# Branch A's last tiles up to w_out: banks of the merged rows, place of the gate chunks' loads, divides and the order of w_out's first half

## The chip, the core and the metric

The kernel runs on one core of a Trainium2 chip. TensorE (PE) multiplies matrices into the eight banks of PSUM; ScalarE (ACT) and VectorE (DVE) read those banks and write SBUF; GpSimd (POOL) works on SBUF; SyncE (SP) issues the DMAs, whose packets are moved by 16 DMA engines. Each engine takes its own instructions in order and waits for the others by semaphores. The metric is the device time of one execution in microseconds.

## The reference

One layer of a bidirectional encoder over 1024 sample rows and 256 prompt rows of width 1024, in fp32. With the checks of masks and padding left out:

```python
h = rmsnorm(x, g_mix); z = h @ w_in
qa, ka, va = ...            # branch A: 8 heads of 64, 2 kv heads, window 128, with a sink
qb, kb, vb = ...            # branch B: 3 groups of 4 heads, dilations 1, 4, 16
gates = sigmoid(z[..., o6:] + b_gate).reshape(b, S, 2, D_MODEL)
o_a, _ = _banded_attention(qa, ka, va, A_WINDOW, 1, rel_bias[:, :A_HEADS], sink)
o_b = _dilated_mixture(qb, kb, vb, rel_bias[:, A_HEADS:])   # mixed by softmax of the groups' lse
merged = gates[:, :, 0] * (o_a @ w_branch_a) + gates[:, :, 1] * (o_b @ w_branch_b)
x = x + merged @ w_out
h = rmsnorm(x, g_mlp)
x = x + square(relu(h @ w_up)) @ w_down
y = rmsnorm(x, g_final)
```

## The kernel before

Rows come in ten tiles of 128 (eight of the sample, two of the prompt) and in three blocks of columns (512, 512, 256). Every product is made from two halves of each operand: a high part rounded to a shorter format by ACT (`hi`, an activation with Copy) and the rest as a low part by DVE (`lo`, a subtraction). `mm3` (L188 to L193) then adds three matmuls to a bank for each pair. PSUM has four kinds of banks: `mm` (3), `sc` (2), `pt` (2) and `pv` (1).

The stages that bear on the change, with their time in the profile: attention A (583 to 769 us), gates and branches (769 to 865), the first half of w_out's columns (865 to 920) and the second half (920 to some 996). Then come the MLP's entry, its up product (from some 1020) and its down product (to the end).

*Attention A* walks 40 steps `i`, one for each of four units and ten row tiles. A step issues the scores of its own tile (L1016 to L1024: matmuls into `sc`, then DVE for the row maximum, ACT for the exponent), the transposes of the tile before into `pt` (L1039), and the values of the one before that (L1053). Between them stand two fillers: `logits` (L1067), which computes five chunks of gate columns with `weight()` and stores them to DRAM (`gs`, `scr_g`), and the merges of branch B. A chunk's weights take three steps: `fetch` (L218) issues the DMA of `raw`, and `prepare` (L224) makes `whi` on ACT (L231) and `wlo` on DVE (L235). `weight()` prepares one chunk ahead of the one that it returns, and fetches within `prepare`. All raw, high and low chunks, the `gs` and the `r` rows come from one ring of ten buffers (`w`).

In steps 36 to 39 `turn_merged` (L1146) transposes a tile of branch B's merged rows into a `pt` bank (L1153) and copies it to `obhi` (ACT, L1161); `low_b` writes `oblo` (DVE, L1165), after which the bank is free. In steps 38 and 40 the weights of branch B are prepared, ahead of that step's scores.

*Gates and branches* are 48 jobs (L1294), each a product for one block and 128 columns into an `mm` bank: first eight of branch B, then four of branch A, for each block, and at the end the other four of branch A. Each is multiplied by a gate (`sg`, loaded from `scr_g` six jobs ahead, L1265; its sigmoid on ACT, L1270) into `mT` on DVE (L1319; for branch A L1321 and L1322). A table `side` (L1286) names what else each job issues: `divide` (L1176, a tile of branch A's rows by its sum), `turn_a` (L1185, its transposes into `pt`), `low_a`, `turn_merged` and `low_b` for the tiles from 4 on.

*w_out* multiplies tile by tile, 24 matmuls each; `part(t)` splits tile t of `mT` into `mhi` (ACT, L185) and `mlo` (DVE, L186), two tiles ahead. DVE adds the bank to the residual `x2`.

What sets the order: up to step 35, and again from job 40 through the first half of w_out, a scheduler orders the instructions of each engine; from step 36 to job 39, and from the second half of w_out on, they stand in the order in which the code issues them (`tc.manual_schedule`).

## Time and profile before

| what | value |
|---|---|
| median of three runs | 1791.44 us (1791.10 to 1794.48) |
| span of the profiled execution | 1788.8 us |
| granted TensorE clock, mean | 0.987 |
| TensorE busy | 1731.5 us (97%) |
| VectorE, ScalarE, GpSimd busy | 991.7, 714.1, 501.6 us |
| HBM read, written | 169.10 MB, 90.73 MB |

The profile's span runs from the first to the last recorded instruction of one execution, and the page has no other time of that execution; the three times are device times of executions without a profile, and their median is 2.64 us above the span. In timeline rows the columns are start and duration in us, engine, line, operation, output and inputs, and in square brackets the idle time ahead of the instruction and what ended it. A row of waits reads: engine, tile and line, what it waited for, then us in total, times and the longest. In a row of windows stand the stretch, its length, the busy time of PE, PEld, DVE, ACT and POOL (instructions in brackets), the granted clock, the mean share of the 16 DMA engines, and GB/s.

### The profile page before, as it was taken

To read this page: it belongs to the slowest core of one execution; us is meant where nothing else is said; L and a number is where in the kernel's file an instruction comes from. 1 tells how busy PE (TensorE), PEld (TensorE's weight loads), DVE (VectorE), ACT (ScalarE), POOL (GpSimd) and SP (SyncE) were. 2 spreads that over 40 slices of the span, in tenths; PEclk is the share of its full clock that TensorE was granted. 3 is DMA by queue.
4 is the path that set the end of the run, shared out by engine and by line. 5 is a ranking of instruction groups with operands and counts; after the bars stand their busy time and mean duration, and the time that the engine had idled before them with its cause. 6 is when DMAs were issued, how large, how long until landed. Compare 5 with 4: busy or idle time off the path is not lost.

```text
span 1788.8 us, 25229 instructions
## 1 busy us (share of the span) xinstructions
PE 1731.5 (97%) x9248; PEld 1466.8 (82%) x9248; DVE 991.7 (55%) x1683; ACT 714.1 (40%) x1531; POOL 501.6 (28%) x396
## 2 busy tenths in 40 slices
PE   7999999999999999999999799999999999999998
PEld 6898888777777889878888688888888788888886
DVE  6623333345545466566737655454554876667575
ACT  6232223344444355454426533333333433333345
POOL 0222321223322111100010255565555451315050
PEclk9999999989999999999999899999999999999999
DMA  6415335555455853164411144433444854623333
GB/s 230 144 37 165 108 105 147 143 147 146 138 161 143 252 158 103 61 241 142 190 47 82 54 140 150 148 118 121 140 150 169 299 199 142 241 95 117 127 113 118
DMA packets 218067, 256.26 MB, mean 143 GB/s; under 512 B 21455, under 2 KB 148771, under 8 KB 217816
## 3 DMA queue, kind: packets, MB, share of 16 engines
q1 hardware_dynamic: 209512, 232.32, 40.4%
q0 software_dynamic: 7344, 20.24, 3.4%
q10 hardware_dynamic: 1088, 2.10, 0.3%
q8 instruction: 73, 1.20, 0.3%
q14 instruction: 50, 0.41, 0.1%
HBM read 169.10 MB, written 90.73 MB: 145 GB/s over the span
## 4 chain that ended last, share of the span: by engine, by line
PE 61%; DVE 3%; ACT 2%; DMA 2%; issue 1%; POOL 0%; SPq 0%; ACTq 0%; DVEq 0%; POOLq 0%
PE dn L344 20%; PE mm L192 13%; PE x L344 10%; PE pv L344 5%; PE z L344 5%; PE y L344 2%; PE pv L1053 2%; PE pt L1039 1%; PE sc L1016 1%; PE sc L1017 1%; PE mm L344 1%; DMA raw<-in_w_down_dram 0%; DVE ulo L186 0%; PE pv L538 0%; DMA raw<-in_w_in_dram 0%
## 5 line engine op out<-in xcount | busy, mean ns | idle before, releaser
L344 PE MATMUL x<-chi,wlo 128*128 128x512 f32 x424 | 172.1, 406 | 6.9 <-ACT phi L185 6.9
L344 PE MATMUL dn<-dhi,ulo 128*128 128x512 f32 x448 | 174.6, 390 | 2.8 <-DVE ulo L186 2.8
L344 PE MATMUL dn<-dhi,uhi 128*128 128x512 f32 x448 | 174.3, 389 | 0.0
L344 PE MATMUL dn<-dlo,uhi 128*128 128x512 f32 x448 | 174.3, 389 | 0.0
L344 PE MATMUL x<-clo,whi 128*128 128x512 f32 x424 | 168.5, 397 | 0.0
L344 PE MATMUL x<-chi,whi 128*128 128x512 f32 x424 | 167.9, 396 | 0.0
L377 POOL TENSOR_TENSOR tb<-raw 128x512 f32<-128x512 f32 x30 | 39.0, 1302 | 453.6 <-PE mm L192 139.6
L311 DVE TENSOR_TENSOR wlo<-ta,whi 128x1024 fp32r<-128x1024 f32 x30 | 56.6, 1887 | 184.7 <-ACT whi L309 184.7
L311 DVE TENSOR_TENSOR wlo<-raw,whi 128x1024 fp32r<-128x1024 f32 x60 | 92.4, 1540 | 105.7 <-ACT whi L309 105.7
L344 PEld LDWEIGHTS dn<-dhi,ulo 128*128 128x128 f32 x448 | 84.1, 188 | 21.4 <-DVE ulo L186 3.8
L344 PEld LDWEIGHTS x<-chi,wlo 128*128 128x128 f32 x424 | 81.8, 193 | 22.9 <-ACT phi L185 7.3
L186 DVE TENSOR_TENSOR ulo<-uraw,uhi 128x1024 fp32r<-128x1024 f32 x56 | 92.0, 1664 | 11.7 <-ACT uhi L185 11.7
L344 PEld LDWEIGHTS dn<-dlo,uhi 128*128 128x128 f32 x448 | 84.1, 188 | 17.4
L344 PEld LDWEIGHTS dn<-dhi,uhi 128*128 128x128 f32 x448 | 84.1, 188 | 17.4
L344 PEld LDWEIGHTS x<-chi,whi 128*128 128x128 f32 x424 | 81.4, 192 | 17.9
L515 ACT ACTIVATE s<-s,o 128x128 f32<-128x128 f32 (+1 forms) x120 | 52.4, 437 | 103.8 <-DVE o L513 55.2
L344 PEld LDWEIGHTS x<-clo,whi 128*128 128x128 f32 x424 | 81.9, 193 | 14.5
L1515 POOL TENSOR_TENSOR t<-raw,t 128x1024 f32<-128x1024 f32 x16 | 47.1, 2959 | 143.3 <-DMA raw<-in_w_down_dram 143.3
L1666 DVE TENSOR_TENSOR v<-v,dn 128x512 f32<-128x512 f32 x90 | 59.6, 683 | 42.6 <-PE dn L344 38.5
L344 PE MATMUL dn<-dhi,up 128*128 128x512 f32 x224 | 73.5, 389 | 0.0
L344 PE MATMUL pv<-phi,wlo 128*128 128x256 f32 x256 | 72.4, 283 | 0.9 <-ACT u L1686 0.9
L344 PE MATMUL z<-chi,wlo 128*128 128x512 f32 x184 | 72.7, 395 | 0.0
(326 smaller groups left out, 4753.0 us busy)
## 6 DMA issues: line engine op xcount, KB each, us to landing
scr_u<-u SPq DMA_DIRECT2D x112, 320.0 KB
uraw<-scr_u SPq DMA_DIRECT2D x56, 512.0 KB
raw<-in_w_in_dram SPq DMA_DIRECT2D x33, 512.0 KB
raw<-in_w_up_dram SPq DMA_DIRECT2D x32, 512.0 KB
raw<-in_w_down_dram SPq DMA_DIRECT2D x28, 512.0 KB
sg<-scr_g SPq DMA_DIRECT2D x32, 256.0 KB
uraw<-scr_u SPq DMA_DIRECT2D x28, 256.0 KB
v<-scr_v SPq DMA_DIRECT2D x96, 64.0 KB
```

What stands on the lines that cost most here:

```text
L186: nc.vector.tensor_tensor(lo, src, hi.bitcast(F32), op=ALU.subtract)
L192: nc.tensor.matmul(ps, a, b, start=i == 0, stop=i == len(seq) - 1)
L311: nc.vector.tensor_tensor(lo, src, hi.bitcast(F32), op=ALU.subtract)
L344: nc.tensor.matmul(ps, a, b, start=first and i == 0, stop=last and i == len(seq) - 1, skip_group_check=True)
L377: nc.gpsimd.tensor_tensor(tb[:, 0], b12, b11, op=ALU.subtract)
L515: nc.scalar.activation(s[:, h, :W], s[:, h, :W], AF.Exp, bias=nm[:, h : h + 1], accum_out=l[:, h : h + 1])
L1016: nc.tensor.matmul(ps[:, :W], q, st["k"][1][:, P * lo : P * lo + W], start=True, stop=False)
L1017: nc.tensor.matmul(ps[:, :W], q, st["k"][0][:, P * lo : P * lo + W], start=False, stop=True)
L1039: nc.tensor.transpose(ps[:, P * (i % 4) : P * (i % 4) + P], s[:, h, P * b : P * b + P], ident)
L1053: nc.tensor.matmul(pv[:, HD * h : HD * h + HD], pt[:, 2 * b + h, :], src, start=b == 0, stop=b == W // P - 1)
L1515: nc.gpsimd.tensor_tensor(o, a, b, op=ALU.subtract)
L1666: nc.vector.tensor_tensor(v, v, ps, op=ALU.add)
```

## The change

1. `prepare` becomes a generator of two steps, the high and the low part. In steps 38 and 40 the high part of branch B's weights is issued after the scores, and the low part after the values.
2. `weight()` also fetches the raw gate chunk that follows the one it has prepared.
3. `turn_merged` takes an `mm` bank for tiles 0 to 3, and an `sc` bank for tiles 4 to 9; tiles 5, 6 and 7 are turned one job sooner.
4. The divides of tiles 4 to 9 stand in jobs 6, 7, 9, 11, 16 and 17 rather than 8, 9, 11, 14, 19 and 21.
5. The code's own order holds from step 36 to the end. `part` of tiles 0 and 1 is issued in jobs 41 and 43. In the first half of w_out a raw chunk of the second half is fetched at tiles 1 to 4 and prepared at tiles 2 to 5, and the second half's parts of tiles 0 and 1 are made at tiles 8 and 9.

```diff
-    def prepare(shared=False):
+    def prepare_steps():
...
+        ready.append((hi, lo))
         nc.scalar.activation(hi, raws[i], AF.Copy)
...
+        yield
+        nc.vector.tensor_tensor(lo, raws[i], hi.bitcast(F32), op=ALU.subtract)
+
+    def prepare():
+        for _ in prepare_steps():
+            pass
...
     def weight(ahead=None):
...
             prepare()
+        while len(raws) < min(len(PLAIN), len(ready) + 1):
+            fetch()
         return ready[i]
...
-        def turn_merged(t):
+        def turn_merged(t, tag="sc"):
...
-            ps = bank("pt")
+            ps = bank(tag)
...
-                last.enter_context(tc.manual_schedule(engines=ALL))
+                ctx.enter_context(tc.manual_schedule(engines=ALL))
             if 36 <= i < 40:
-                turn_merged(i - 36)
-            if i in (38, 40):
-                prepare()
+                turn_merged(i - 36, "mm")
...
+            if i in (38, 40):
+                weights_b = prepare_steps()
+                next(weights_b)
             if 36 <= i < 40:
                 low_b(i - 36)
...
                 values_of(*order[i - 2])
                 tick(3 * i + 2)
+            if i in (38, 40):
+                next(weights_b, None)
...
-                3: [(low_b, 4), (turn_a, 2)], 4: [(low_a, 2), (turn_a, 3)], 5: [(low_a, 3), (turn_merged, 5)],
-                6: [(low_b, 5), (turn_merged, 6)], 7: [(low_b, 6), (turn_merged, 7)], 8: [(low_b, 7), (divide, 4)],
...
+                3: [(low_b, 4), (turn_a, 2)], 4: [(turn_merged, 5), (low_a, 2), (turn_a, 3)],
+                5: [(low_b, 5), (turn_merged, 6), (low_a, 3)], 6: [(divide, 4), (low_b, 6), (turn_merged, 7)],
+                7: [(divide, 5), (low_b, 7)], 9: [(turn_a, 4), (divide, 6)], 10: [(low_a, 4), (turn_a, 5)],
...
-            if i == 40:
-                last.close()
             load_gate(i + 6)
+            if i in (41, 43):
+                part(i // 43, 0)
...
                 if hh == 0:
                     nc.vector.tensor_tensor(x2[t][:, sl], x2[t][:, sl], ps, op=ALU.add)
-                    part(t + 2)
+                    part(t + 2, hh)
                     if 2 <= t < 6:
                         prepare()
+                    if 0 < t < 5:
+                        fetch()
+                    if t > 7:
+                        part(t - 8, 1)
                     elif t in (6, 7):
                         next(more)
```

Three places show how the instructions move. On SP, at the start of attention A: `q`, `qp`, `vp` are loads of branch A's operands, `gs` a finished piece of gate logits, `r` the rows for a merge. Before:

```order
L418 DMA q<-scr_qa_110 128x1024 x2
L431 DMA qp<-scr_qa_109 128x256 x2
L434 DMA vp<-scr_v 128x2x128
L1076 DMA scr_g_137<-gs 128x512
L431 DMA qp<-scr_qa_110 128x256 x2
```

and, after two more stores of `gs` and sixteen loads of `r`, the next chunk:

```order
L1076 DMA scr_g_137<-gs 128x512
L222 DMA raw<-in_w_in_dram 128x8x128
L413 DMA kk<-scr_ka 64x1024
L414 DMA kp<-scr_ka 64x256
L413 DMA kk<-scr_ka 64x1024
L1086 DMA r<-scr_b__81 128x1x132
```

Now:

```order
L422 DMA q<-scr_qa_110 128x1024 x2
L435 DMA qp<-scr_qa_109 128x256 x2
L438 DMA vp<-scr_v 128x2x128
L222 DMA raw<-in_w_in_dram 128x8x128
L1080 DMA scr_g_137<-gs 128x512
```

The chunk's DMA moved ahead of the stores of `gs` and the loads of `r`; the chunk after it now stands where this one stood, and the loads of `kk` and `kp` follow eight and more loads of `r` later.

On DVE, in step 38 (`s,m` and `m` are the scores' maximum, `nm_a` its negative, `pv` the values). Before:

```order
L264 COPY o<-pv 128x128
L235 TENSOR_TENSOR wlo<-raw,whi 128x1024
L1018 ISA s,m<-sc,bias 128x256
L1018 ISA m 128x1
L1018 ISA s,m<-sc,bias 128x256
L1018 ISA m 128x1
L1022 SCALAR_TENSOR_TENSOR nm_a<-m,nsink 128x2
L1165 TENSOR_TENSOR oblo_0_7476<-pt,obhi_0_7475 128x128 x2
```

Now:

```order
L268 COPY o<-pv 128x128
L1022 ISA s,m<-sc,bias 128x256
L1022 ISA m 128x1
L1022 ISA s,m<-sc,bias 128x256
L1022 ISA m 128x1
L1026 SCALAR_TENSOR_TENSOR nm_a<-m,nsink 128x2
L1169 TENSOR_TENSOR oblo_0_7476<-mm,obhi_0_7475 128x128 x2
L268 COPY o<-pv 128x128
L234 TENSOR_TENSOR wlo<-raw,whi 128x1024
```

`oblo` reads an `mm` bank, and `wlo` stands behind the step's scores, `oblo` and values rather than ahead of them.

On DVE, at the last jobs (from 40 on) and w_out's first tile (`sg` and `mT` are a job's two products). Before:

```order
L1321 TENSOR_TENSOR sg<-mm,sg 128x256
L1322 TENSOR_TENSOR mT_1_8294<-mT_1_8294,sg 128x256
L186 TENSOR_TENSOR mlo<-mT_0_7816,mhi 128x256
L186 TENSOR_TENSOR mlo<-mT_1_7817,mhi 128x256
L186 TENSOR_TENSOR mlo<-mT_2_7818,mhi 128x256
L186 TENSOR_TENSOR mlo<-mT_3_7819,mhi 128x256
```

Now:

```order
L1341 TENSOR_TENSOR mT_2_8083<-mT_2_8083,sg 128x512
L186 TENSOR_TENSOR mlo<-mT_0_7816,mhi 128x256
L186 TENSOR_TENSOR mlo<-mT_1_7817,mhi 128x256
L186 TENSOR_TENSOR mlo<-mT_2_7818,mhi 128x256
L186 TENSOR_TENSOR mlo<-mT_3_7819,mhi 128x256
L1340 TENSOR_TENSOR sg<-mm,sg 128x512
L1341 TENSOR_TENSOR mT_2_8083<-mT_2_8083,sg 128x512
```

The four low parts of a tile stood behind the last job's products, and now stand between the products of two earlier jobs.

## The prediction

> **What bounds the kernel.** I read the shares first, then the granted clock by slice, then TensorE's waits in the stages that the diff touches, then the timeline around each of those waits.

> ```profile
> span 1788.8 us, 25229 instructions
> PE 1731.5 (97%) x9248; PEld 1466.8 (82%) x9248; DVE 991.7 (55%) x1683; ACT 714.1 (40%) x1531; POOL 501.6 (28%) x396
> PEclk9999999989999999999999899999999999999999
> ```

> TensorE is busy for 97% of the span, and no other engine for more than 55%. The change takes no matmul away, so all that it can win lies in TensorE's idle moments and in the stretches at a lower clock. The second 8 (slice 23, 983.8 to 1028.6 us) is the entry to the MLP, which the diff does not touch. The waits of TensorE from 560 us to 960 us (us in total, times, longest), in the answers for 560 to 760, 760 to 860 and 860 to 960:

> ```profile
> PE pt L1039 <- ACT s L1024: 3.6, 1, 3.6
> PE pt L1039 <- DVE oblo L1165: 2.0, 2, 1.1
> PE pt L1153 <- DVE oblo L1165: 1.9, 1, 1.9
> ...
> PE pt L1153 <- DVE oblo L1165: 2.3, 1, 2.3
> PE pt L1185 <- DVE o L1176: 1.4, 2, 0.8
> ...
> PE mm L192 <- DVE mlo L186: 1.3, 1, 1.3
> ```

> That is 3.6 + 2.0 + 1.9 + 2.3 + 1.4 + 1.3 = 12.5 us in eight waits, and each part of the change stands beside one of the rows.

> **Gate chunk fetched ahead.** The longest wait is a transpose of scores that waits for ACT, and ACT had stood at the high half of a gate chunk, which waited for its DMA:

> ```profile
> 620.58 0.43 SPq L222 DMA_DIRECT2D raw<-in_w_in_dram  x1
> 628.17 1.06 ACT L231 ACTIVATE whi<-raw 128x1024 fp32r<-128x1024 f32 x1 [4.51 <-DMA raw<-in_w_in_dram]
> 629.13 0.60 ACT L1024 ACTIVATE s<-s,nm_a 128x384 f32<-128x384 f32 x1
> 629.88 1.04 PE L1039 MATMUL pt<-ident,s 128*128 128x128 f32 x4 [3.56 <-ACT s L1024]
> ...
> 630.00:632.00 2.00, 2.00 (x11) 2.00 (x12) 1.69 (x8) 0.60 (x1) 0.00 (x0) 0.50 0.36 106
> 632.00:634.00 2.00, 2.00 (x8) 1.72 (x8) 0.00 (x0) 1.45 (x6) 0.54 (x1) 0.65 0.03 7
> ```

> The raw chunk took 628.17 − 620.58 = 7.6 us to arrive. Now its DMA stands right behind the `vp` load, which SP issued here at 604.99:

> ```profile
> 604.99 0.44 SPq L434 DMA_DIRECT2D vp<-scr_v  x1
> ...
> 628.10 0.58 SPq L1086 DMA_DIRECT2D r<-scr_b__81  x1
> ```

> That is 15 us sooner, three times the 4.51 us that ACT waited, so TensorE's 3.56 go. In the two windows behind it (the number ahead of the last two is the granted clock) the clock is 0.50, then 0.65: half speed up to about 633.4, or 3.5 us, in which 1.7 us of work was lost. Sum: 3.56 + 1.7 = 5.3 us. The lower bound is 0, if the earlier DMA finds no free buffer. What is late next: loads of `kk` and `kp` go behind 8 to 16 more of the small `r` loads on SP, at 0.58 us each 5 to 9 us; they belong to the unit that starts ten steps later, and I put this at nothing (if that cover were gone, a wait of up to 9 us). Later chunks gain the same lead.

> **Merged rows in the matmul banks.** Rows of `merged` and the transposed scores share two `pt` banks, and a bank comes free only when `oblo` is written. The third wait shows why that is late:

> ```profile
> 747.22 1.06 ACT L231 ACTIVATE whi<-raw 128x1024 fp32r<-128x1024 f32 x1
> 748.31 1.23 DVE L235 TENSOR_TENSOR wlo<-raw,whi 128x1024 fp32r<-128x1024 f32 x1 [3.26 <-ACT whi L231]
> 749.45 0.42 DVE L1018 CUSTOM_DVE_ANT_0 s<-sc,bias 128x256 f32<-128x256 f32 x1
> 750.33 0.48 DVE L1165 TENSOR_TENSOR oblo<-pt,obhi 128x128 fp32r<-128x128 f32 x2
> 750.96 0.41 PE L1153 MATMUL pt<-ident,merged 128*128 128x128 f32 x2 [1.91 <-DVE oblo L1165]
> ...
> 748.00:750.00 2.00, 1.05 (x10) 0.91 (x9) 1.69 (x4) 0.28 (x1) 0.00 (x0) 1.00 0.00 0
> 752.00:754.00 2.00, 2.00 (x13) 1.66 (x12) 0.99 (x7) 1.70 (x8) 0.00 (x0) 1.00 0.10 33
> ```

> `oblo` stood behind the 1.23 us of `wlo` and the scores. After the change the four turned tiles lie in three `mm` banks, of which the open gate sum holds one; each of the other two is asked for again two tiles later, a whole step after its `oblo`, and `wlo` stands behind the values. So all three waits go: 2.0 + 1.9 = 3.9 us, with no clock term, since the clock stayed at 1.00 here. The bounds are 2.0, if the last wait only changes its bank, and 3.9.

> **Job stage.** The turn of row tile 7 waits 2.30 us, and jobs 7 and 8 queue behind it on TensorE.

> ```profile
> 779.89 0.72 ACT L1270 ACTIVATE sg<-sg,bg 128x512 f32<-128x512 f32 x1 [0.87 <-DMA sg<-scr_g]
> 780.52 1.04 ACT L231 ACTIVATE whi<-raw 128x1024 fp32r<-128x1024 f32 x1
> 781.27 0.40 PE L192 MATMUL mm<-obhi,whi 128*128 128x512 f32 x1
> 781.60 1.23 DVE L235 TENSOR_TENSOR wlo<-raw,whi 128x1024 fp32r<-128x1024 f32 x1 [1.89 <-ACT whi L231]
> 782.74 0.68 DVE L1319 TENSOR_TENSOR mT<-mm,sg 128x512 f32<-128x512 f32 x1
> 783.97 0.66 PE L1153 MATMUL pt<-ident,merged 128*128 128x128 f32 x2 [2.30 <-DVE oblo L1165]
> 786.99 0.42 PE L192 MATMUL mm<-ohi,wlo 128*128 128x512 f32 x1
> ...
> 784.00:786.00 2.00, 2.00 (x6) 1.71 (x7) 0.81 (x3) 1.05 (x3) 0.00 (x0) 0.50 1.03 374
> 786.00:788.00 2.00, 2.00 (x8) 1.53 (x8) 0.80 (x2) 1.67 (x2) 0.00 (x0) 0.75 1.05 385
> ```

> In an `sc` bank, and a job sooner, the turn waits for nothing. Job 7 (six matmuls at some 0.23 us) then runs to about 783.2, where job 8 meets its own wait: its bank is freed by the `mT` that ends at 782.74 + 0.68 = 783.42, behind `wlo`. Some 0.2 to 0.9 us stay; I take 0.5. The half clock lasted from 783.6 to 787.0 (0.50, then 0.75), again 3.4 us, and cost 1.7. Sum: 2.30 + 1.7 − 0.5 = 3.5 us. The lower bound is 0, since ACT here waits for the gate logits' DMA (0.87), with the 16 engines full, and a DMA gets no faster; the upper bound is 4.0.

> [...]

> **Divides ahead, and w_out's first parts ahead.** The two waits for a divide (1.4 us) go when each divide stands two to five jobs sooner. The wait for `mlo` (1.3 us) is the queue at the stage's end: eight of its pieces must precede the first sums, and they began only behind the last job's products.

> ```profile
> 865.04 6.12 DVE L186 TENSOR_TENSOR mlo<-mT,mhi 128x256 fp32r<-128x256 f32 x18
> 850.00:860.00 10.00, 10.00 (x53) 8.56 (x52) 6.78 (x11) 7.68 (x19) 0.00 (x0) 1.00 0.91 353
> ```

> Moved into jobs 41 and 43 they cost VectorE 8 × 0.34 = 2.7 us in a stretch where it is busy for 6.78 of 10: 9.5 of 10 then. Behind them on VectorE stand the products that free TensorE's banks, and three banks give a slack of two jobs. It is enough on paper and has no air. For this, and for small waits elsewhere, I take off as much as the two divide waits cost, 1.4 us (bounds 0 and 4: one wait like the longest with no clock loss).

> **The sum.** 5.3 + 3.9 + 3.5 + 1.4 + 1.3 = 15.4, less 1.4: 14.0 us. In the profiled execution 1788.8 − 14.0 = 1774.8. The median shown lies 2.64 us above that span, so I forecast 1791.44 − 14.0 = 1777.4. With all upper bounds it is 15.9 us less (1775.5); a neighbouring small wait that goes with these could add 2 (1773.5). With one of the two large terms halved and the deduction at 4, the gain is about 9 (1782).

> **Rivals.**
> 1. *The waits move.* The ring that holds raw, high and low chunks has ten buffers. If none is free at the new place, SP holds the DMA, with the `gs` stores and `r` loads behind it, and the 5.3 us stay; or the gate logits' DMA sets the job stage, and its 3.5 + 1.4 stay. Against the first: at 604.99 SP issues with 15 us in hand. For the second: a DMA share of 1.03 and 1.05. Either gives about −9 us, 1783; both −4, 1787.
> 2. *The clock has its own phase.* If the half-speed stretch at 783.6 is no result of that stall, its 1.7 us stay: 1779.1. For it: the 1.91 us stall had none. Against it: both stretches begin with the stalls. [...]
> 3. *A later stage takes the gain.* The MLP's entry could wait for something that does not come sooner. Against it: the chain of waits runs through TensorE's tiles of w_out into that entry. 1791, no change.
> 4. *The written order turns on itself.* In w_out's first half the four chunks of the second half now have fixed places on ACT, each between the `mhi` of two tiles. Ahead of the first of them ACT had waited for a DMA, and a tile of w_out takes TensorE 5.48 us:

> ```profile
> 870.41 1.07 ACT L231 ACTIVATE whi<-raw 128x1024 fp32r<-128x1024 f32 x1 [4.61 <-DMA raw<-in_w_out_dram]
> ...
> 931.99 5.48 PE mm L192 x24
> ...
> 866.00:880.00 14.00, 14.00 (x64) 11.54 (x63) 13.91 (x31) 6.63 (x12) 0.00 (x0) 1.00 0.47 175
> ```

> ACT works one tile ahead, so TensorE is touched once a chunk arrives over 5.5 us behind its place; at 10 us late each costs 4.5 + 1.7 for the clock, four of them 25 us: 1777.4 + 25 = 1802, slower. Against it: the DMA engines are under half used (0.47), and each chunk is fetched a tile before its use.
> 5. *It doesn't do what it says.* Were the turned rows still held in their new banks until the same `oblo`, the 3.9 us would stay: 1781. The four tiles are a step apart, which speaks against it.

> **Chances.** The forecast 0.58, the waits moved 0.22, the clock's phase 0.06, the banks 0.03, no change 0.06, slower 0.05. The forecast's own range is 1774 to 1781; with the moved waits the range is 1773.5 to 1786.5. Below 0.2% (3.6 us) a measurement of this kernel, whose three times span 3.4 us, tells nothing. Faster by more: 0.58 + 0.22 + 0.06 + 0.03, less 0.03 for both halves of rival 1 failing together, 0.86. Within 0.2%: 0.06 and those 0.03, less 0.01, 0.08. Slower: 0.06.

> **What would show it.** In the profile after, TensorE's waits for `s`, for `oblo` and for `mlo` should be missing from these stages, and the `whi` of the gate chunks should not wait for a DMA; the granted clock should read 1.00 where it was 0.50. The slices of the MLP should be as long as before, and its entry should still wait some 10 us. I am wrong if a wait for `mT`, `sg` or a `whi` of w_out over 2 us stands in their place, if the first gate chunk's `whi` still waits, or if the MLP takes longer.

## The result, and the profile after

The changed kernel takes 1774.48 us (median; 1771.84 to 1774.84) where the kernel before takes 1791.27 us (1789.38 to 1794.48 with one run more than shown ahead). The ratio is 0.9901, with an interval of 0.9885 to 0.9916: faster by some 17 us. The forecast was 1777.4 us, 14.0 less. The head of the page of the changed kernel:

```profile
span 1770.1 us, 25230 instructions
PE 1721.5 (97%) x9248; PEld 1460.5 (83%) x9248; DVE 999.4 (56%) x1683; ACT 712.6 (40%) x1531; POOL 500.2 (28%) x396
PEclk9999999999999999999999999999999999999999
```

TensorE's waits from 560 to 960 us, eight before, are down to one:

```profile
PE mm L192 <- DVE mT L1338: 1.1, 1, 1.1
```

The first gate chunk to be fetched early no longer waits on ACT (no bracket behind the row). The chunk ahead of it, whose load did not move, waits 3.76 us there before and after, and TensorE does not wait for it. In the stretch from 600 to 650 us TensorE is busy throughout (first number behind the comma; granted clock third from the end). The row of the changed kernel's timeline, then that stretch before, then after:

```profile
612.48 1.04 ACT L232 ACTIVATE whi<-raw 128x1024 fp32r<-128x1024 f32 x1
...
600.00:650.00 50.00, 46.44 (x317) 43.11 (x316) 29.68 (x114) 22.63 (x68) 5.45 (x10) 0.97 0.60 171
...
600.00:650.00 50.00, 50.00 (x350) 46.27 (x350) 36.91 (x145) 27.79 (x85) 6.52 (x12) 1.00 0.61 178
```

Both kernels have the same 9248 matmuls in nearly the same order, so one can compare the time from one matmul's start to a later one's start. I cut the program at matmuls that stand on either side of a part of the change (numbers in TensorE's order), and read both starts from the two timelines:

| stretch (matmuls) | before, us | after, us | difference |
|---|---|---|---|
| start to 3150: through attention B | 577.05 | 572.96 | −4.1 |
| 3300 to 3600: gate chunk of steps 10 to 15 | 48.01 | 42.62 | −5.4 |
| 4200 to 4450: steps 36 to 39, into the jobs | 43.26 | 38.62 | −4.6 |
| 4450 to 4490: to job 8 | 12.08 | 9.32 | −2.8 |
| 4560 to 4650: divides of tiles 4 and 5 | 20.67 | 18.71 | −2.0 |
| 4800 to 4950: last jobs, start of w_out | 30.50 | 29.19 | −1.3 |
| 5450 to 5600: the MLP's entry | 43.04 | 41.75 | −1.3 |
| 7500 to 7650: entry of the down product | 34.10 | 36.80 | +2.7 |

All other stretches agree within 0.1 us, and with them w_out from matmul 4950 on, so the new places of its chunks and of the second half's first parts show neither a gain nor a loss. The five stretches of the change give 5.4 + 4.6 + 2.8 + 2.0 + 1.3 = 16.1 us. The other three rows, together 2.7 us, lie where the program is the same; the experiments show what they are.

### The profile page after: what moved, and what is told of

It reads as the page before. It is cut to its first block, busy times and chain, and to the rows that moved or that the text cites. A ratio compares the mean times of both kernels' runs of the same rounds, so it can differ in the third digit from the quotient of the medians.

```text
span 1770.1 us, 25230 instructions
## 1 busy us (share of the span) xinstructions
PE 1721.5 (97%) x9248; PEld 1460.5 (83%) x9248; DVE 999.4 (56%) x1683; ACT 712.6 (40%) x1531; POOL 500.2 (28%) x396
## 4 chain that ended last, share of the span: by engine, by line
PE 63%; DVE 3%; ACT 2%; DMA 1%; issue 1%; POOL 0%; SPq 0%; DVEq 0%; ACTq 0%; POOLq 0%
PE dn L348 20%; PE mm L192 13%; PE x L348 10%; PE pv L348 5%; PE z L348 5%; PE pv L1057 2%; PE y L348 2%; PE pt L1043 1%; PE sc L1020 1%; PE sc L1021 1%; DVE ulo L186 1%; PE mm L348 1%; DMA raw<-in_w_down_dram 0%; PE pv L542 0%; DVE clo L315 0%
## 5 line engine op out<-in xcount | busy, mean ns | idle before, releaser
L186 DVE TENSOR_TENSOR ulo<-uraw,uhi 128x1024 fp32r<-128x1024 f32 x56 | 98.4, 1776 | 11.7 <-ACT uhi L185 11.7
```

The lines of the kernel that those rows point to most:

```text
L186: nc.vector.tensor_tensor(lo, src, hi.bitcast(F32), op=ALU.subtract)
```

## The experiments

Each kernel below is the changed one with one part undone, unless it says otherwise. Times are compared with the kernel before, which had 1789.4 to 1791.6 us in these series.

**The gate chunk's load, undone**

```diff
-        while len(raws) < min(len(PLAIN), len(ready) + 1):
-            fetch()
```

> The changed kernel without the earlier fetch of the raw gate chunk; all else as changed. My theory: the wait of a score transpose for ACT comes back (3.6 us idle, then some 3.4 us at a granted clock of 0.50), so TensorE reaches step 15 of attention A 5.3 us later than in the changed kernel, and the time is 5.3 us more, about 1780. The rival 'the waits move' (a later stage has its own limit, so that a shift in attention A is taken up there): TensorE is later in attention A, but the time is within 2 us of the changed kernel's. The rival 'the clock has its own phase': idle 3.6 us without a half-speed stretch behind it, 1778.

1778.09 us, ratio 0.9932 (0.9917 to 0.9947). TensorE's wait is back, and the windows around it show the clock (the stretches are laid along its windows, 3.413 us long in the records of the last section; TensorE's busy time is the first number behind the comma, the granted clock the third from the end):

```profile
PE pt L1041 <- ACT s L1026: 4.0, 1, 4.0
...
622.30:625.70 3.40, 0.08 (x1) 0.00 (x0) 0.00 (x0) 1.04 (x2) 0.00 (x0) 1.00 0.79 170
625.70:629.10 3.40, 2.73 (x13) 2.73 (x14) 2.51 (x8) 1.21 (x4) 0.00 (x0) 0.51 0.30 85
629.10:632.50 3.40, 3.40 (x9) 2.63 (x10) 0.00 (x0) 1.57 (x6) 0.54 (x1) 0.50 0.06 19
```

The stretch of matmuls 3300 to 3600 takes 49.70 us, 7.1 more than in the changed kernel: 4.0 idle, and this time nearly two windows at half speed, 3.1 us. The stretch to job 8 behind it takes 8.70 us, 0.6 less than in the changed kernel; it takes from 8.7 to 10.1 us in the nine profiles whose turns and weights stand as in the changed kernel, so this may be chance. So the part pays its own gain, and nothing later takes up more than 0.6 us of it; its size is 5 to 7 us: behind the wait of 3.6 us in the kernel before the clock read 0.50 for one window (3.4 us), behind this one of 4.0 us for nearly two. In the time of the whole 3.6 us of it are seen, less than the 5.3 expected, where the times of one kernel span 3 us and more.

**The gate chunk's load alone, put into the kernel before**

```diff
             prepare()
+        while len(raws) < min(len(PLAIN), len(ready) + 1):
+            fetch()
         return ready[i]
```

> The kernel before with nothing but the earlier fetch of the raw gate chunk. My theory: 5.3 us less than before, about 1786, with the waits at steps 36 to 39, in the job stage (2.3, 1.4) and at w_out (1.3) as before, the half-speed stretch behind the 2.3 us too, at its new time. The rival 'the clock has its own phase': the 2.3 us wait stays, but the clock behind it reads 1.00, since all of it comes 5.4 us sooner. If the later stages had taken up the gain: 1790.

1786.25 us, ratio 0.9969 (0.9956 to 0.9982): 5.3 us less than the kernel before in the same series (1791.59). The stretch 3300 to 3600 takes 42.62, as in the changed kernel, and all later waits are there:

```profile
PE pt L1155 <- DVE oblo L1167: 1.9, 1, 1.9
PE pt L1155 <- DVE oblo L1167: 2.7, 1, 2.7
PE pt L1187 <- DVE o L1178: 1.4, 2, 0.9
PE mm L192 <- DVE mlo L186: 1.3, 1, 1.3
```

One thing was not expected by either theory. The wait of 1.9 us, behind which the clock stayed at 1.00 in the kernel before, has 0.50 behind it here. The windows around that wait, of this kernel and then of the kernel before:

```profile
739.20:742.60 3.40, 1.49 (x14) 1.38 (x14) 2.67 (x9) 1.22 (x4) 0.00 (x0) 1.00 0.00 0
742.60:746.00 3.40, 3.40 (x12) 2.82 (x11) 1.42 (x7) 2.64 (x10) 0.54 (x1) 0.50 0.06 19
...
746.10:749.50 3.40, 2.95 (x25) 2.68 (x23) 1.19 (x2) 1.39 (x3) 0.00 (x0) 1.00 0.06 19
749.50:752.90 3.40, 1.94 (x12) 1.75 (x13) 2.70 (x16) 2.15 (x8) 0.54 (x1) 1.00 0.06 19
752.90:756.30 3.40, 3.40 (x23) 2.97 (x22) 0.85 (x3) 2.56 (x7) 0.54 (x1) 1.00 0.26 90
```

Here the whole wait lies in one window (TensorE busy 1.49 of 3.4 us), there a border cuts it (2.95 and 1.94). The stretch 4200 to 4450 takes 44.83 us, 1.6 more than in the kernel before, with the same waits.

**The merged rows: the bank alone, and the low part alone, undone**

```diff
-                turn_merged(i - 36, "mm")
+                turn_merged(i - 36, "pt")
```

> The changed kernel with row tiles 0 to 3 turned in the pt banks again, the low parts of the weights still late. If the bank is the cause: waits of some 4 us on oblo come back at steps 36 to 39 (two of 1 us, one of 1.9), and the time is about 4 us more than the changed kernel's. If the late low part alone does it: only the two waits of 1 us come back, 2 us more, and the third (1.9 us) stays away, since nothing of 1.23 us stands ahead of that oblo.

```diff
+            if i in (38, 40):
+                prepare()
...
-            if i in (38, 40):
-                weights_b = prepare_steps()
-                next(weights_b)
...
-            if i in (38, 40):
-                next(weights_b, None)
```

(in the second, `prepare()` stands ahead of the scores)

> The changed kernel with both halves of branch B's weights prepared ahead of the scores of steps 38 and 40 again, the rows still turned in mm banks. If the bank is the cause: no wait of TensorE at steps 36 to 39, and the time of the changed kernel within 1 us. If the late low part matters by itself: a wait of 1 to 2 us for scores or oblo at step 39.

With the `pt` banks 1776.31 us (ratio 0.9922, 0.9905 to 0.9939), with the early low part 1773.73 (0.9908, 0.9893 to 0.9922). The waits of the first, and then of the second:

```profile
PE pt L1043 <- DVE oblo L1169: 2.0, 2, 1.1
...
PE sc L1020 <- DVE m L1022: 0.7, 1, 0.7
PE mm L192 <- DVE oblo L1169: 0.2, 1, 0.2
```

In the first the two waits of 1 us are back and the third is not; in the second none of the three is back, but 0.9 us of others. The stretch 4200 to 4450 takes 41.04 and 40.06, against 38.62 with both and 43.26 with neither. So the bank takes two of the waits away, and either of the two edits takes the third. The late low part alone leaves 2.4 of the 4.6 us, the bank alone 1.4. The times of the whole (1776.31 and 1773.73 against 1774.48) can't tell this; the stretches do.

**The turns of the job stage, undone**

```diff
-        def turn_merged(t, tag="sc"):
+        def turn_merged(t, tag="pt"):
...
-                3: [(low_b, 4), (turn_a, 2)], 4: [(turn_merged, 5), (low_a, 2), (turn_a, 3)],
-                5: [(low_b, 5), (turn_merged, 6), (low_a, 3)], 6: [(divide, 4), (low_b, 6), (turn_merged, 7)],
-                7: [(divide, 5), (low_b, 7)], 9: [(turn_a, 4), (divide, 6)], 10: [(low_a, 4), (turn_a, 5)],
+                3: [(low_b, 4), (turn_a, 2)], 4: [(low_a, 2), (turn_a, 3)],
+                5: [(low_a, 3), (turn_merged, 5)], 6: [(divide, 4), (low_b, 5), (turn_merged, 6)],
+                7: [(divide, 5), (low_b, 6), (turn_merged, 7)], 8: [(low_b, 7)], 9: [(turn_a, 4), (divide, 6)], 10: [(low_a, 4), (turn_a, 5)],
```

> The changed kernel with row tiles 4 to 9 turned in pt banks and at their old jobs, divides as changed. My theory: the wait of 2.3 us ahead of job 7 comes back, with a stretch of 3.4 us at a clock of 0.50 behind it, and job 8 starts 2.9 to 3.5 us later against job 0 than in the changed kernel; the time is some 3 us more, 1777 to 1778. The rival 'the clock has its own phase': the wait comes back but at this other moment the clock stays at 1.00, so about 1.7 us less than that. The rival 'the gate logits' DMA sets the stage': job 8 starts at the same distance from job 0 as in the changed kernel, and the time is the same.

1777.43 us, ratio 0.9931 (0.9914 to 0.9947).

```profile
PE pt L1157 <- DVE oblo L1169: 3.0, 1, 3.0
...
770.80:774.20 3.40, 1.25 (x7) 1.11 (x8) 3.40 (x9) 0.89 (x4) 0.00 (x0) 1.00 1.06 380
774.20:777.60 3.40, 3.40 (x10) 2.62 (x9) 2.42 (x5) 1.80 (x3) 0.00 (x0) 0.50 1.06 389
```

The stretch 4450 to 4490 takes 12.86 us, 3.5 more than in the changed kernel. Wait and half speed are both back, the wait 11 us sooner in the execution than in the kernel before. So the gate logits' DMA does not fix job 8's place, though the engines are as full (1.06). The run undoes the bank and the earlier job together; which of the two takes the wait away is not shown.

**What is left ahead of job 8.** In the changed kernel the remaining wait looks like this:

```profile
766.37 0.72 ACT L1276 ACTIVATE sg<-sg,bg 128x512 f32<-128x512 f32 x1 [1.27 <-DMA sg<-scr_g]
767.00 1.04 ACT L232 ACTIVATE whi<-raw 128x1024 fp32r<-128x1024 f32 x1
768.07 1.23 DVE L234 TENSOR_TENSOR wlo<-raw,whi 128x1024 fp32r<-128x1024 f32 x1 [1.89 <-ACT whi L232]
769.21 0.68 DVE L1338 TENSOR_TENSOR mT<-mm,sg 128x512 f32<-128x512 f32 x1
770.04 0.47 PE L192 MATMUL mm<-ohi,wlo 128*128 128x512 f32 x1 [1.09 <-DVE mT L1338]
```

`mT`, which frees the bank, stands behind `wlo`, this behind `whi`, and this on ACT behind a sigmoid that waits for its DMA. One run moves the weights ahead of the sigmoid:

```diff
-            open_gate(i + 3)
             if i in (1, 4, 22, 26):
                 fetch()
...
+            open_gate(i + 3)
             hi, lo = w_bs[c // 4] if x == "b" else w_as[c // 2]
```

> The changed kernel with the weights of a job issued ahead of the gate's sigmoid of that job, so that the high part of w_a no longer stands behind a sigmoid that waits for its DMA. If that order makes the remaining wait ahead of job 8 (1.1 us there for mT, behind the low part of w_a): the wait goes, job 8 starts 1 us sooner, 1 us less in all, not to be told from no change by the time. If the raw chunk itself comes no sooner: ACT waits for it ahead of the sigmoid, and job 8 starts as before or later.

1773.59 us, ratio 0.9909 (0.9892 to 0.9926). No wait for `mT` of 0.15 us or more is left: the stretch 4450 to 4490 takes 8.33 us, where the changed kernel had 9.32, and 9.89 in its second profile. But ACT now waits for the raw chunk itself:

```profile
770.55 1.06 ACT L232 ACTIVATE whi<-raw 128x1024 fp32r<-128x1024 f32 x1 [0.90 <-DMA raw<-in_w_branch_a_dram]
```

That gain of 1 to 1.6 us in the stage (0.4 to 1.8 against the nine profiles that leave those turns and weights alone) can't be told from nothing in the time of the whole.

**The divides, undone** (tiles 4 to 9 in jobs 8, 9, 11, 14, 19 and 21)

```diff
-                5: [(low_b, 5), (turn_merged, 6), (low_a, 3)], 6: [(divide, 4), (low_b, 6), (turn_merged, 7)],
-                7: [(divide, 5), (low_b, 7)], 9: [(turn_a, 4), (divide, 6)], 10: [(low_a, 4), (turn_a, 5)],
...
+                5: [(low_b, 5), (turn_merged, 6), (low_a, 3)], 6: [(low_b, 6), (turn_merged, 7)],
+                7: [(low_b, 7)], 8: [(divide, 4)], 9: [(turn_a, 4), (divide, 5)], 10: [(low_a, 4), (turn_a, 5)],
...
```

> The changed kernel with the divides of tiles 4 to 9 at their old jobs. My theory: the two waits of turn_a for a divide come back, 1.4 us in all, with no loss of clock; TensorE reaches w_out 1.4 us later against job 0, and the time is 1.4 us more, which three rounds may not tell from no change. If the divides ahead cost something in the jobs that they now stand in (they stand ahead of the products that free the banks): the wait of 1.1 us for mT ahead of job 8 is shorter or gone, and the loss is under 1 us.

1778.59 us, ratio 0.9926 (0.9912 to 0.9941).

```profile
PE pt L1189 <- DVE o L1180: 1.3, 2, 0.8
```

The stretch 4560 to 4650 takes 20.67 us, 2.0 more, and to the hundredth what it took in the kernel before. The wait for `mT` was not shorter without the divides (1.6 us), so they do not cause it. The time is 4 us above the changed kernel's; the rest of that is in the stretches that no edit touched (below).

**The parts of w_out, undone, and the scheduler's order, put back**

```diff
-            if i in (41, 43):
-                part(i // 43, 0)
...
+            if hh == 0:
+                part(0, 0)
+                part(1, 0)
```

> The changed kernel with the parts of row tiles 0 and 1 made behind the last job, in the written order to the end. My theory: the wait for mlo at w_out's first sum comes back, 1.3 us or a little more (in the written order all eight pieces stand behind the last products), and no wait appears in jobs 41 to 47 either way; 1.3 to 2.5 us more. Rival (VectorE has no air in those jobs): jobs 41 to 47 run faster by up to 1 us, so that the loss is near nothing.

The other run puts the scheduler back from job 40 to the end of w_out's first half:

```diff
-                ctx.enter_context(tc.manual_schedule(engines=ALL))
+                last = ctx.enter_context(ExitStack())
+                last.enter_context(tc.manual_schedule(engines=ALL))
...
+            if i == 40:
+                last.close()
...
+            if hh:
+                ctx.enter_context(tc.manual_schedule(engines=ALL))
```

> The changed kernel with the scheduler's order again from job 40 through w_out's first half, the parts of tiles 0 and 1 still issued in jobs 41 and 43. If the place of the parts in the code is what took the wait away: no wait at w_out's start, time within 1 us. If the written order is: the scheduler puts the pieces behind the last products again and the wait of 1.3 us is back. Rival 4 of the prediction (the written order costs in w_out's first half): this kernel is faster than the changed one.

The late parts took 1775.69 us (ratio 0.9911, 0.9895 to 0.9928), with their wait back, and the stretch 4800 to 4950 at 30.93 us, 1.7 more:

```profile
PE mm L192 <- DVE mlo L186: 1.5, 1, 1.5
```

With the scheduler's order there is no wait at w_out, and that stretch takes 28.90 us, 0.3 less than the written order. So the parts' place in the code takes the wait away, and the written order gains nothing there. The time was 1771.10 us (ratio 0.9887, 0.9869 to 0.9906), which looked like rival 4 in small. The last series tests it, together with the weights ahead of the sigmoid:

> The same, and the scheduler's order from job 40 through w_out's first half as in the run scheduled_end. If the written order there costs something (rival 4, small): 1 to 3 us below the changed kernel and below the run before this one. If the lower time of scheduled_end was chance: the same as the run before this one within 1.5 us, since TensorE's stages differed by 0.3 us only.

1773.39 us, ratio 0.9904 (0.9883 to 0.9925), against 1773.59 without the scheduler's order, and 1773.98 for the changed kernel in the same series. The 3 us of the run scheduled_end did not come back and are put down to chance; neither variant can be told from the changed kernel.

**The changed kernel again**

> The changed kernel once more, for its time beside the next two and for a second profile. If the differences of up to 3 us between profiles in attention B, at the MLP's entry and at the entry of the down product come from the clock's grid and not from the change, they come out otherwise here while the stages of the change repeat to 0.1 us outside the job stage. Time within 2 us of 1774.5.

1773.98 us, ratio 0.9912 (0.9892 to 0.9932), and in the second profile the stretches of the change repeat to 0.1 us (42.71, 38.62, 18.71, 29.18), but for the one to job 8 (9.89). The MLP's entry takes 43.92 us this time, and the entry of the down product 34.05, so neither the −1.3 nor the +2.7 of the table belongs to the change. The entry of the down product was 33.9 to 34.6 us in all other profiles. In the first profile of the changed kernel, the rows of that place show a longer wait and VectorE slower at the very same work, with a sum on GpSimd beside it; below them, the same rows of the second profile:

```profile
PE dn L348 <- DVE ulo L186: 4.7, 2, 3.1
1374.27 5.83 POOL L1521 TENSOR_TENSOR t<-raw 128x1024 f32<-128x1024 f32 x2 [3.39 <-DMA raw<-in_w_down_dram]
1374.48 6.71 DVE L186 TENSOR_TENSOR ulo<-uraw,uhi 128x1024 fp32r<-128x1024 f32 x2
...
PE dn L348 <- DVE ulo L186: 2.0, 2, 1.7
1376.70 4.54 DVE L186 TENSOR_TENSOR ulo<-uraw,uhi 128x1024 fp32r<-128x1024 f32 x2
1376.94 6.55 POOL L1521 TENSOR_TENSOR t<-raw 128x1024 f32<-128x1024 f32 x2 [3.85 <-DMA raw<-in_w_down_dram]
```

In the first profile GpSimd's instruction starts 0.21 us ahead of the first `ulo`, and that `ulo` takes 3.38 us. In each of the 13 others `ulo` starts first, by 0.2 to 0.6 us, and takes 1.22 us; the second `ulo`, which always starts while GpSimd works, takes 3.4 us in all 14. So the 2.7 us go with the order of two instructions on two engines, and the same kernel has it one way and the other. Why VectorE's instruction is the longer one then is not shown; no run changes the order on purpose.

Attention B (matmuls 1650 to 3150), which no edit touches, took from 244.8 to 248.6 us over the 14 profiles. TensorE's waits there add up to 12.4 to 12.7 us in 13 of them (13.5 in the other), but the windows at half speed number from four to seven: with four the stage took 244.8 to 245.9 us, with seven 248.3 to 248.6. The kernel before has seven and the changed kernel four, which goes with 3.7 of the −4.1 us in the table's first row. Here is one place, a wait of 1.0 and one of 0.8 us, in the kernel before and then in the changed kernel:

```profile
490.10:493.50 3.40, 1.55 (x9) 0.74 (x7) 1.78 (x3) 1.99 (x6) 2.28 (x3) 1.00 0.02 5
493.50:496.90 3.40, 3.40 (x13) 2.36 (x11) 2.18 (x8) 1.04 (x5) 0.92 (x2) 0.50 0.26 93
...
485.70:489.10 3.40, 2.38 (x13) 1.49 (x11) 2.85 (x2) 0.79 (x5) 3.32 (x4) 1.00 0.28 74
489.10:492.50 3.40, 2.57 (x14) 1.75 (x15) 2.30 (x7) 1.59 (x5) 0.98 (x2) 1.00 0.08 25
```

Before, both waits fell into one window, and the next ran at half speed; in the changed kernel a border parted them, and none did.

**Stalls of set lengths**

```diff
+            for _ in range({6: 4, 12: 5, 17: 6, 23: 7, 29: 9}.get(10 * u + t, 0)):
+                nc.scalar.activation(a3("jk", (P, 3 * P), 1)[:, :W], s[:, 1, :W], AF.Copy)
             for h in range(2):
                 nc.scalar.activation(
                     s[:, h, :W], s[:, h, :W], AF.Exp,
```

> The changed kernel with extra copies of the scores on ACT (0.5 to 0.6 us each, into a tile that nobody reads) ahead of the exponents of steps 6, 12, 17, 23 and 29 of attention A: 4, 5, 6, 7 and 9 of them, so that TensorE stands idle there for lengths that grow from about 1 us to about 4 us. The output is not touched. Theory A (grid): the clock is set window by window on a grid of 3.41 us whose place in an execution is its own, and a window in which TensorE is busy for less than about 45% puts the next one at 0.50. So a wait under 1.9 us never halves the clock, one over 3.7 us always does, and one between does or doesn't by where the grid cuts it; each half window costs 1.7 us. Theory B (the length of the wait alone): all waits from 2.3 us on halve the clock and none under it does. [...]

This run told nothing on its question. The 31 copies ran (0.5 us each, from 626.9 to 716.0 us), but no wait of TensorE appeared from 580 to 760 us: the scheduler had room for them ahead of the exponents. The time of the one run was 1773.69 us. What the theories say of the clock was then read from all 14 profiles, which hold enough stalls of their own (last section).

## Why the prediction was right, point by point

**Direction, place and mechanism held.** The five terms were each taken away at the place and by the instruction that the prediction named, and each comes back where its part is undone. The measured time lies 2.9 us below the forecast and inside the range, though near its lower end (1774); the second series' 1773.98 touches that end. Of the signs, the MLP's entry still waits 6.9 and 3.2 us, before and after alike. The clock reads 1.00 where it read 0.50, and no wait of TensorE over 2 us stands in place of the old ones. One sign failed in a harmless way: the `whi` of one gate chunk still waits for its DMA (the 3.76 us above).

**Gate chunk ahead: 5.3 forecast, 5.4 measured.** The extra lead was enough, and the loads of `kk` and `kp` that were pushed back cost nothing to be seen.

**Merged rows in the matmul banks: 3.9 forecast, 4.6 measured.** The row of waits gave 3.9; the starts of the matmuls around them give 0.7 us more, mostly because the next matmul comes later than the wait's row says: by 1.31, 1.05 and 2.08 us for waits of 1.14, 0.89 and 1.91. The prediction credited the bank and the late low part together, and this holds: neither alone reaches it.

**Job stage: 3.5 forecast, 2.8 measured.** The wait for `mT` that was to remain was 1.1 us (1.7 in the second profile, and from 0.5 to 1.9 in the nine profiles named above), not 0.5. Its mechanism was the one named, `mT` behind `wlo`. ACT's wait for the gate logits' DMA stood in the prediction as a reason for the lower bound only; in the sum it was not allowed to grow, and it grew from 0.87 to 1.27 us. That this miss of 0.7 us and the one above cancel is luck.

**Divides 1.4 and parts 1.3 forecast, 2.0 and 1.3 measured.** The two listed waits for a divide made the next start 1.00 and 0.67 us later, and a third gap, too short to be listed (0.08 us), made 0.24.

**The mis-sized term is the deduction.** The prediction took off 1.4 us, because VectorE would have no air in the last jobs. VectorE did get as full as it worked out (9.56 of 10 us, 9.5 forecast), but TensorE was busy throughout (TensorE is the first number behind the comma, VectorE the third):

```profile
830.00:840.00 10.00, 10.00 (x48) 8.37 (x47) 9.56 (x18) 5.59 (x13) 0.00 (x0) 1.00 0.73 272
```

No new wait appeared there; with the parts moved back behind the jobs nothing in the jobs got faster. Without the deduction the five terms give 15.4, and 1791.44 − 15.4 = 1776.0; as measured they give 16.1, and 1775.3. The last 0.8 us to the median lie within what runs of one kernel differ by.

**Rivals.** The waits did not move (1): job 8 came sooner, and at most the 0.6 us above were given back. The clock's own phase (2) was half right. The half-speed stretch does belong to the stall, against this rival: with the turns undone it came back behind the wait, 11 us sooner. But a stall of one length does not bring one each time: behind the wait of 1.9 us at steps 36 to 39 the clock read 1.00 in the kernel before, where TensorE was busy for 2.95 and 1.94 us of the two windows that shared it, and 0.50 in the kernel with only the early load, where it was busy for 1.49 us of the one. The 1.7 us at the job stage was therefore a likely cost and not a certain one. So the contrast of the stall of 2.30 us, which had half speed behind it, with that of 1.91 us, which had none, makes no threshold. No later stage took the gain (3). The written order cost nothing that can be told (4): ACT waits 4.4 us for the first chunk of w_out, 4.6 before, and TensorE does not. The banks did what they were to do (5).

## What to carry to other kernels

Where one engine is busy for 97% of the time, list the few waits that it has and trace each to the instruction that was early in the wrong queue; here a DMA one chunk sooner, other banks and a few moved instructions gave 16 us without any work taken away. Compare two profiles by the distance between the same matmuls rather than by their spans: an effect of 1 us is then seen in one profile, where the times of whole runs differ by 3 and more. When two edits remove one wait, undo each alone before crediting either.

## What the runs showed of the hardware

How busy TensorE was ahead of a 0.50 is worked out from the records of the clock and TensorE's busy intervals, between 60 and 1750 us, for windows that ran at full speed, with busy shares rounded to whole per cents. In the 14 profiles all 64 windows in which TensorE was busy for less than 46% were followed by one at 0.50; of those from 46% to 59%, 26 were and 28 were not; of those from 60% on, none. The profiles before and after alone have ten of the first kind, from 0% to 43%, all followed by 0.50; of the second, four that were (46%, 50%, 54%, 54%) and five that were not (47%, 48%, 49%, 51%, 56%); and 951 of the third. What decides between 46% and 59% is not shown.

A window at 0.50 costs up to 1.7 us, half of its 3.413. So one stall of 1.9 us (kernel before 1.00, with only the early load 0.50), or two of 1.0 and 0.8 us close together (kernel before 0.50, changed kernel 1.00), may or may not cost that on top, and the same program differs by some microseconds from run to run: in its second series the changed kernel took 1771.81 us at a mean granted clock of 0.993 and 1779.59 us at 0.987.
